# Channel mean and pointwise product of a convolution branch, from plain fp32 to rounded products of high and low parts

## The chip, the cores and the metric

One Trainium2 chip, and on it one core. The metric is the device time of one execution in microseconds (us), the median of the runs shown. A core has a matmul engine (TensorE, PE in the profile, with its weight loads as PEld), three engines for elementwise work (VectorE: DVE, ScalarE: ACT, GpSimd: POOL) and SyncE (SP), whose queue issues all transfers (DMAs) of this kernel.

## What is computed

The reference is a step of a two-layer mixer for 512 prompt tokens and 8 decoding sequences with one token each, 520 columns in all, with a model width of 1024. Each layer has a convolution branch, a pooling branch and three kinds of attention (compressed, selected, window). What matters here is the convolution branch: a depthwise convolution of width 31 over 256 channels, a layer norm over the channels, SiLU, and a pointwise product with a 256 x 256 matrix.

```python
def layernorm(x, g, b):
    mu = jnp.mean(xf, axis=-1, keepdims=True)
    xc = xf - mu
    var = jnp.mean(xc * xc, axis=-1, keepdims=True)
    return (xc * lax.rsqrt(var + EPS) * g + b)

def conv_mixer(u, buf, w_dw, b_dw, ln_g, ln_b, w_pw, b_pw):
    y = lax.conv_general_dilated(xcat, w_dw[:, None, :], ...)
    y = layernorm(y + b_dw, ln_g, ln_b)
    y = jax.nn.silu(y) @ w_pw + b_pw

def mixer_output(...):
    y = jnp.concatenate([y_a * jax.nn.silu(z_a), y_b * jax.nn.silu(z_b), o * jax.nn.silu(z_c)], axis=-1)
    return x + (y @ w_out)
```

## The kernel before

Activations lie with channels on the 128 partitions and the 520 tokens in columns, so a tile is 128 x 520, and 256 channels are two tiles. A matmul works on half of the columns, 260 (`HALF`).

The kernel has two forms of product. The large ones (`product`, lines 744 to 753; 24 per layer for the input projection, 8 for the output) are *rounded*: each operand is split into a high part, which is a copy in the rounded format fp32r, and a low part, the rest (`split`, lines 724 to 726, two operations). A burst of six matmuls then forms high x high, high weight x low activation and low weight x high activation, for both halves of the columns. The small ones, among them both products of the convolution branch, are plain fp32: one matmul per half, no split. In the trace a plain fp32 matmul stands as two records, a rounded one as one.

`conv_norm` (lines 1070 to 1101) is the branch behind the convolution. The channel mean is a product with `mean_w`, a fixed tile filled with 1/256, so that each partition gets the mean of all 256 channels; it takes one burst of two matmuls for each of the two channel tiles. The mean is subtracted, the square summed over channels by another product, the reciprocal root formed and spread by a DMA over DRAM, then come scale, tanh (for SiLU) and the pointwise product: two output tiles `m`, two channel tiles `c`, a burst of two matmuls each.

Which engine runs which elementwise operation, and in which order all of it is issued, is written out in the table `TUNE`. Wherever the program calls `ch("svg").copy(...)` and the like, the next letter of the string `engines` names the engine: `v` VectorE, `s` ScalarE, `g` GpSimd (756 letters). The program first writes down all its instructions, in bursts that stay together, and numbers the bursts as they come; the list `order` (3309 numbers) then says in which order they are issued. Each engine takes its own in that order, and a tile's place is taken from the tiles that are free at that point, so a late reader holds back a later writer. SP's transfers are in the same list.

Step names in this document are those of the program's list of steps per layer: `k`, `v` and `q` are projections to keys, values and queries, `za` and `zc` gates, `w` the output projection, `cn` is `conv_norm`. The warm-up products are in `constants` (lines 629 to 633): 12 bursts of two plain matmuls of `mean_w` with itself, whose result nobody reads. Their numbers are 3 to 14; the memset of `mean_w` is 2, the eight loads of x are 16 to 23, and 35 is the square of the first tile of x, 36 the sum of it on TensorE.

Of the kernel before, what the change touches and what calls it, by code (L numbers as in the profile page):

```python
# [9 lines left out]
F32R = mybir.dt.float32r  # L10
# [179 lines left out]
class Plan:  # L190
# [135 lines left out]
    def emit(self, tc, ctx):  # L326
# [60 lines left out]
        "vvvvgvvsssssvssgsvvggvggsvsvvssvvsgvvssvsvggsvvvgvgssgsggvvvgvsgsgsgvvggvvvsvvvvvssvsvsvsgggsvvvsvsgvgvsvgvgvssv"  # L387
        "vvsgsgsvssgvvsggsvgvsgsvsvggsvsggsvvggvggggvvssgvsssvsvsvggvvsgsgvggvvgvvgsssssggggssssvssssssvgvvggvvsvsvsgsgvv"
        "vsvvsvgsvvgvggssvvssvsvvvsvgvggggsgsvvgggggsvgvgvsssgvssvsssssvssssvsssgggvvvggsvgvvvvgvgsssssvvssvvsvvsgvvggsgg"
        "ggvggvvgvgsvvvvgsgsvvvsvgvsvsgvgsgsvsvsvsvggsvsgssggssvsvvvgvvgvgvggsvvsssvsvsssvssvgvvsssggggggvgvvvgsgsvvgssvg"  # L390
        "vsvgvsvvgsvssggvvsvgvvgvvggvsvvvvsvgvgvssvggsvvvsvssvgvsgvggvgsvggsgsgsgvgggvsggggvvvssgsvsvvsvsvsgggsgggvggvggs"
        "gsggssggssssvgsssvsvssvsgggsgvvsggvggvggvsggvssvsgvsgggssssvssvsvvvsssgvvggvggsgvvsssgggvgvgvsssssssssvsvvsvvsss"
        "sgvgvgvgvgvgvvvggvssvvvvssgvsvsvvsggvsgggvvsgsggvvsgsvgvsgggsggvsgggsgsgsvsvsvsvggvv"
    ),
    "order": (
# [146 lines left out]
def step_kernel(ctx: ExitStack, tc: tile.TileContext, i, o, tune=None):  # L542
# [82 lines left out]
    def constants():  # L625
        ve.memset(ones, 1.0)
        sc.activation(junk, ones[:, :1], AF.Exp)
        ve.memset(mean_w, 1.0 / 256.0)
        warm = plan.bank("warm", "t")
        for n in range(WARM // 2):  # L630
            with plan.burst():
# [85 lines left out]
    def layer(l):  # L717
        z_ = Layer()
# [824 lines left out]
```

## Time and profile before

| | us |
|---|---|
| median of 3 runs | 624.89 (624.7 to 625.42) |
| the profiled execution | 623.73 |
| its span, first to last instruction | 622.0 |
| TensorE busy in it | 606.4 |
| VectorE busy | 433.7 |
| ScalarE busy | 259.7 |
| GpSimd busy | 226.2 |

The profile shows one execution. An engine's busy time is that in which at least one of its instructions ran; matmuls overlap, so the time from the start of one row to the start of the next tells more than a row's own length. All rows have the line L352, the helper that issues every operation, so they are told apart by engine, names and shapes: `banks` is a result of TensorE, `t` a tile in the pools, `keep` a fixed tile, `small` a small one.

### The profile page before, as it was taken

How to read it: one execution, taken by the hardware profiler on the slowest of the kernel's cores; microseconds unless marked ns; L12 is line 12 of the kernel's file. 1: busy time of each engine (PE TensorE's matmuls, PEld its weight loads, DVE VectorE, ACT ScalarE, POOL GpSimd, SP SyncE). 2: the span in 40 equal slices, each digit the busy share in tenths (PEclk: the TensorE clock that was granted, in tenths of full speed). 3: DMA queues.
4: the chain of work that ended last, by engine and by line, in shares of the span. 5: the costliest groups of instructions: out<-in, count | busy, mean ns of one | idle time of the engine just before them, and what ended most of it. 6: DMA issues, size and time to landing. Idle time of an engine off the chain costs nothing.

```text
span 622.0 us, 15002 instructions
## 1 busy us (share of the span) xinstructions
PE 606.4 (97%) x5526; PEld 536.7 (86%) x5526; DVE 433.7 (70%) x1222; ACT 259.7 (42%) x731; POOL 226.2 (36%) x250
## 2 busy tenths in 40 slices
PE   6999999999999999999999999999999999999997
PEld 5999998898868788579999999999985968677997
DVE  6535879966778697965465498887677678688221
ACT  4102125656683395431221132237575769543100
POOL 2123225442414363341522242556443535144700
PEclk9999999999999999999999999999999999999999
DMA  8755444322652346887546234342246135788622
GB/s 267 217 166 180 152 124 146 115 76 73 136 122 65 104 125 220 268 252 228 185 143 194 85 113 160 94 124 62 77 79 155 37 95 140 185 255 252 208 77 95
DMA packets 89130, 90.98 MB, mean 146 GB/s; under 512 B 25858, under 2 KB 59746, under 8 KB 88930
## 3 DMA queue, kind: packets, MB, share of 16 engines
q1 hardware_dynamic: 89058, 90.04, 48.9%
q8 instruction: 43, 0.70, 0.5%
q14 instruction: 29, 0.24, 0.1%
HBM read 75.32 MB, written 14.67 MB: 145 GB/s over the span
## 4 chain that ended last, share of the span: by engine, by line
PE 84%; DVE 6%; SPq 5%; DMA 3%; issue 2%; ACT 1%; ACTq 0%; DVEq 0%
PE banks L352 84%; DVE t L352 4%; SPq L352 3%; DVE small L352 2%; DMA t<-in_win 2%; SPq L616 1%; ACT t L352 1%; DMA t<-in_x 1%; DMA t<-in_cmp 0%; DVE keep L352 0%; ACTq L352 0%; DVEq L352 0%
## 5 line engine op out<-in xcount | busy, mean ns | idle before, releaser
L352 PE MATMUL banks<-t,t 128*128 128x260 f32 (+5 forms) x3960 | 490.0, 302 | 1.9 <-DVE t L352 0.8
L352 PEld LDWEIGHTS banks<-t,t 128*128 128x128 f32 (+3 forms) x3960 | 434.2, 178 | 32.8 <-issue 25.1
L352 POOL TENSOR_TENSOR t<-t,t 128x512 fp32r<-128x512 f32 (+4 forms) x84 | 111.4, 1332 | 129.2 <-PE banks L352 55.7
L352 ACT ACTIVATE t<-t 128x512 fp32r<-128x512 f32 (+4 forms) x130 | 78.5, 613 | 155.1 <-DVE t L352 56.8
L352 ACT ACTIVATE t<-t,small 128x384 f32<-128x384 f32 (+4 forms) x185 | 99.2, 552 | 16.2 <-DVE small L352 15.9
L352 PE MATMUL banks<-keep,t 128*128 128x128 f32 (+7 forms) x698 | 87.2, 311 | 1.9 <-DVE t L352 1.1
L352 DVE TENSOR_TENSOR t<-t,t 128x512 fp32r<-128x512 f32 (+3 forms) x92 | 71.0, 782 | 22.0 <-PE banks L352 16.0
L352 PEld LDWEIGHTS banks<-keep,t 128*128 128x128 f32 (+2 forms) x698 | 66.5, 161 | 22.1 <-issue 12.5
L352 DVE TENSOR_TENSOR t<-banks,t 128x520 f32<-128x520 f32 (+1 forms) x54 | 37.2, 693 | 63.8 <-PE banks L352 51.2
L352 DVE CUSTOM_DVE_ANT_0 t<-banks,keep,small 128x384 f32<-128x384 f32 (+3 forms) x128 | 64.3, 528 | 16.2 <-PE banks L352 16.0
L352 POOL TENSOR_SCALAR t<-t 128x512 fp32r<-128x512 f32 (+2 forms) x49 | 34.6, 707 | 88.3 <-PE banks L352 48.5
L352 ACT ACTIVATE t<-banks 128x512 f32<-128x512 f32 (+3 forms) x72 | 36.6, 525 | 62.1 <-PE banks L352 45.7
L352 PE MATMUL banks<-t,keep 128*32 128x130 f32 (+7 forms) x688 | 41.2, 306 | 6.7 <-DVE keep L352 4.8
L352 PEld LDWEIGHTS banks<-t,keep 128*32 128x32 f32 (+3 forms) x688 | 23.2, 116 | 20.5 <-DVE keep L352 5.0
L352 POOL TENSOR_SCALAR t<-t,small 128x384 f32<-128x384 f32 (+3 forms) x50 | 32.9, 671 | 21.2 <-DVE small L352 15.4
L352 ACT ACTIVATE small<-small 128x32 f32<-128x32 f32 (+3 forms) x76 | 23.5, 310 | 27.5 <-DVE small L352 27.4
L352 DVE COPY t<-banks 128x512 f32<-128x512 f32 (+2 forms) x37 | 21.5, 589 | 11.2 <-PE banks L352 7.3
L352 DVE SCALAR_TENSOR_TENSOR t<-t,t 128x520 f32<-128x520 f32 (+2 forms) x32 | 27.8, 873 | 1.3 <-ACT t L352 1.1
L352 POOL TENSOR_TENSOR t<-t,keep 128x520 f32<-128x520 f32 (+1 forms) x11 | 14.2, 1296 | 33.5 <-DVE t L352 20.4
L352 POOL TENSOR_TENSOR t<-t 128x520 f32<-128x520 f32 (+1 forms) x12 | 12.8, 1068 | 33.2 <-DVE t L352 13.9
L352 ACT ACTIVATION_READ_ACCUMULATOR t<-t,small 128x1 f32 x132 | 24.7, 187 | 0.0
L352 DVE SCALAR_TENSOR_TENSOR small<-small 128x130 f32<-128x130 f32 (+3 forms) x80 | 23.5, 296 | 1.5
(81 smaller groups left out, 358.1 us busy)
## 6 DMA issues: line engine op xcount, KB each, us to landing
t<-in_w_in SPq DMA_DIRECT2D x96, 256.0 KB
t<-in_cmp SPq DMA_DIRECT2D x64, 128.0 KB
t<-in_slc SPq DMA_DIRECT2D x64, 128.0 KB
t<-in_w_out SPq DMA_DIRECT2D x32, 256.0 KB
t<-in_x SPq DMA_DIRECT2D x16, 260.0 KB
t<-in_win SPq DMA_DIRECT2D x16, 256.0 KB
out_win<-t SPq DMA_DIRECT2D x16, 256.0 KB
t<-glu SPq DMA_DIRECT2D x12, 264.0 KB
```

Source lines behind the costliest of these rows:

```text
L352: fn(*[real(v) for v in o.a], **{k: real(v) for k, v in o.k.items()})
L616: pages[n] = tc.nc.sync.value_load(pt.real(plan)[0:1, n:n + 1], min_val=0, max_val=n_phys - 1)
```

## The change

Both products of the branch are made rounded ones. For the mean, 1/256 is exact in the rounded format, so there is one weight tile, `mean_r` (a copy of `mean_w`), and two passes, for the high and the low part of the activations: four matmuls of 260 columns per channel tile in place of two. For the pointwise product the weights and the activations after SiLU are split, and a burst of six matmuls takes the place of two. That adds per layer five splits: the weights, two activation tiles ahead of the mean and two ahead of the pointwise product, 10 elementwise operations with a letter each. With `mean_r`, the numbers of all bursts after 2 rise by one; the warm-up bursts are now 4 to 15.

Both lists are written anew: `engines` (now 776 letters) with v 315 (before 274), s 256 (251), g 205 (231), and `order` (3330 numbers). The new order begins with the memset of `mean_w` and has eleven of the twelve warm-up bursts ahead of every other work of TensorE; the number of transfers is the same, 473.

```diff
     "order": (
-        "78 16 35 0 36 15 27 33 17 79 2 3 4 18 34 37 80 19 39 81 84 22 40 5 6 21 115 38 82 43 57 47 20 44 48 7 41 85 59 "
...
+        "2 4 5 17 6 7 16 79 36 8 81 9 34 10 116 35 82 0 11 12 13 28 18 14 118 119 38 39 19 40 20 42 43 37 48 85 24 370 21 "
...
+    mean_r = new("c", [128, 128], F32R, fixed=True)
...
         ve.memset(mean_w, 1.0 / 256.0)
+        ve.tensor_copy(mean_r, mean_w)
...
         def conv_norm():
             yv = z_.conv
+            z_.cy = []
             raw = new("wpw", [128, 2, 256])
             ld(raw, i["w_pw"][l])
+            wh, wl = (new("wpw", [128, 2, 256], F32R) for u in "hl")
+            split(raw, wh, wl, "gv")
             pm = plan.bank("pm", "mm", 2)[:, :, :T // 2]
             for c in range(2):
+                parts = [P("cy", F32R) for u in "hl"]
+                split(yv[c], *parts)
                 with plan.burst():
-                    for k, (a, b) in enumerate(HALF):
-                        te.matmul(pm[:, k], mean_w, yv[c][:, a:b], start=(c == 0), stop=(c == 1))
+                    for n, v in enumerate(parts):
+                        for k, (a, b) in enumerate(HALF):
+                            te.matmul(pm[:, k], mean_r, v[:, a:b], start=(c == n == 0), stop=(c == n == 1))
...
                 ve.scalar_tensor_tensor(yv[c], t, 1.0, yv[c], op0=OP.add, op1=OP.mult)
+                parts = [P("cy", F32R) for u in "hl"]
+                split(yv[c], *parts)
+                z_.cy.append(parts)
             for m in range(2):
                 pm = plan.bank("pm", "mm", 2)[:, :, :T // 2]
-                for c in range(2):
+                for c, (yh, yl) in enumerate(z_.cy):
                     with plan.burst():
-                        for k, (a, b) in enumerate(HALF):
-                            te.matmul(pm[:, k], raw[:, c, 128 * m:128 * m + 128], yv[c][:, a:b], start=(c == 0), stop=(c == 1))
+                        for n, (w, v) in enumerate(((wh, yh), (wh, yl), (wl, yh))):
+                            for k, (a, b) in enumerate(HALF):
+                                te.matmul(pm[:, k], w[:, c, 128 * m:128 * m + 128], v[:, a:b],
+                                          start=(c == n == 0), stop=(c == 1 and n == 2))
                 finish(m, pm, pcol(V_BPW + m), OP.add)
```

## Rows read from the trace of the kernel before

**Rows 1.** The page: busy time of each engine, and the chain that ended last.

```profile
PE 606.4 (97%) x5526; PEld 536.7 (86%) x5526; DVE 433.7 (70%) x1222; ACT 259.7 (42%) x731; POOL 226.2 (36%) x250
...
PE 84%; DVE 6%; SPq 5%; DMA 3%; issue 2%; ACT 1%; ACTq 0%; DVEq 0%
```

**Rows 2.** Busy time by stretch: stretch, its us, engines (instructions), clock, DMA share, GB/s.

```profile
8.00:11.00 3.00, 3.00 (x19) 2.15 (x19) 3.00 (x5) 1.27 (x2) 2.62 (x2) 1.00 1.02 363
...
61.00:93.00 32.00, 31.99 (x268) 31.33 (x266) 26.43 (x68) 7.13 (x17) 8.66 (x11) 1.00 0.48 145
93.00:125.00 32.00, 30.58 (x308) 27.57 (x309) 29.74 (x110) 19.07 (x56) 16.48 (x16) 1.00 0.41 127
...
340.00:430.00 90.00, 90.00 (x805) 85.69 (x804) 72.46 (x221) 28.61 (x85) 37.49 (x35) 1.00 0.36 115
```

**Rows 3.** PE's timeline at the start: start, us, shape, count, idle before and its releaser.

```profile
4.82 0.66 PE L352 MATMUL banks<-t,keep 128*32 128x130 f32 x8 [4.82 <-DVE keep L352]
...
9.02 0.66 PE L352 MATMUL banks<-t,keep 128*32 128x130 f32 x8
9.61 1.75 PE L352 MATMUL banks<-keep 128*128 128x128 f32 x8
11.28 0.65 PE L352 MATMUL banks<-t,keep 128*32 128x130 f32 x16
...
12.33 1.68 PE L352 MATMUL banks<-t,t 128*128 128x260 f32 x12
...
18.12 0.61 PE L352 MATMUL banks<-keep 128*128 128x128 f32 x4
18.48 1.68 PE L352 MATMUL banks<-t,t 128*128 128x260 f32 x12
...
31.62 0.43 PE L352 MATMUL banks<-t,keep 128*32 128x130 f32 x8 [1.03 <-POOL t L352]
32.68 10.33 PE L352 MATMUL banks<-t,t 128*128 128x160 f32 x82 [0.64 <-DMA t<-in_cmp_w]
```

**Rows 4.** DVE's timeline at the start, and SP's issues (us of issuing).

```profile
4.03 0.70 DVE L352 TENSOR_TENSOR t<-t 128x520 f32<-128x520 f32 x1 [4.03 <-DMA t<-in_x]
...
5.11 0.17 DVE L352 MEMSET keep<- 128x128 f32 x1
...
0.75 0.39 SPq L352 DMA_DIRECT2D t<-in_w_in  x1
...
33.51 7.12 SPq L352 DMA_DIRECT2D t<-in_cmp  x7
```

**Rows 5.** PE's timeline at the mean (layer one) and the pointwise product (layer two).

```profile
197.95 1.92 PE L352 MATMUL banks<-t,keep 128*128 128x260 f32 x8
199.80 0.96 PE L352 MATMUL banks<-keep,t 64*128 64x512 f32 x6
...
530.15 1.04 PE L352 MATMUL banks<-t,t 128*128 128x260 f32 x4
531.03 1.04 PE L352 MATMUL banks<-keep,t 128*128 128x128 f32 x8
```

**Rows 6.** PE's timeline: rounded products alone and in a long run.

```profile
446.85 0.96 PE L352 MATMUL banks<-t,t 128*128 128x260 f32 x6
447.65 0.60 PE L352 MATMUL banks<-keep,t 128*128 128x128 f32 x4
...
576.90 41.23 PE L352 MATMUL banks<-t,t 128*128 128x260 f32 x342
```

**Rows 7.** Groups by form, DVE and POOL: count, busy us, mean ns, idle before.

```profile
L352 DVE TENSOR_TENSOR t<-t,t 128x512 fp32r<-128x512 f32 x76 | 60.6, 804 | 21.8 <-PE banks L352 16.0 <-POOL t L352 3.1 <-issue 1.2
...
L352 DVE CAST t<-t 128x512 fp32r<-128x512 f32 x27 | 12.4, 464 | 4.0 <-DMA t<-in_w_in 3.6 <-PE banks L352 0.3
...
L352 POOL TENSOR_TENSOR t<-t,t 128x512 fp32r<-128x512 f32 x68 | 91.9, 1355 | 116.0 <-PE banks L352 55.3 <-ACT t L352 33.2 <-DVE t L352 16.5
```

**Rows 8.** The last piece of the chain: start, us, what.

```profile
618.17 0.70 DVE t L352
```

More of the change, by code (lines that the diff above doesn't have):

```diff
@@ L386 @@
     "engines": (
[L387 to L393, printed above, removed]
+        "vsssvvssgsssgssssvsgsgvvsgvgsvsssvgvvsgvvgggssvvvssvgvsvvvvvsvvvvvsvvvvvgvvsvvvvvssgggsvvvvgsggvsvssgvvsvsgsgssg"
+        "vvsgggsvssvvvsggsvsvvgsvsvsvggsgssvggvvvggsssgsvvsvsvggvgggsvsvvvvgsvsvsgvgsvggsvvgggssssssvsvvggsggvsgggggvsgsg"
+        "gvssvgvgvgsvsgvsvsvvssssssssgvgsvsvgvgvvvvvgvvvvgvssggggsgsvsgsvgvsssvssvsssssssssgsggvvvgvvvggvvvssvvsvvvgsssss"
+        "vsvsvsvsgsgggsvgvgvvgvsgsvsvvvvvsgsvvgvvsvvgvvsvvvvvsssvvgvvsvgsvvsvsgvgsgvvsggvvgssvsvvvggsvvggsssvvvggggsgvvvv"
+        "svvvsvsvvsvsgvvgvvgvvssvvvvssgvvvgvvsgvvvgvsggvsvsvvvvsggvsvssvvvsvvgvgggvsvsvsgsgggvsssvgsvssvvgvvvvvsssvvvgsgg"
+        "gsvggggvgsggvvssgvvsgsvgsvvsvsssvsvggsvvgvsggvvgvgsggsvssgssgsggssssvvssssvssvvvgggsvgvggggvgsvvvsggvgggssssvgsv"
+        "svggsvvvvsssvvsvssvvssvvvgvggvvgvggvggssvssvsgsvssvssvvsggvvgvvsvgvvvvvgsgsvsgsvsvsvgvsgggsvvgsggvgvsgsg"
     ),
     "order": (
[140 rows of a table removed]
[141 rows of a table added]
     ),
```

279 rows, old and new, of the table TUNE are left out of this document.

## The prediction

> **What bounds the kernel now.** I read the page first [rows 1]. TensorE (PE) is busy 97% of the span, VectorE (DVE) 70%, ScalarE (ACT) 42%, GpSimd (POOL) 36%, and the chain of work that ended last lies on PE for 84%. So a change pays if it shortens PE's own queue or takes away one of PE's waits; work on the other engines costs something only where PE has to wait for it. "Busy" hides two things. In a long run of rounded products 342 matmuls of 260 columns take 41.23 us, 0.12 us each, or 0.72 us for a burst of six [rows 6]; near other work the same burst takes 0.80 us (446.85 to 447.65, rows 6). And the first 12 us are slow: PE does nothing for 4.82 us, and then a burst of two warm-up products (four records) takes 0.84 us (9.61 to 11.28 is two bursts), while a later one takes 0.36 us (18.12 to 18.48) [rows 3]. [...] The end is short: the last sum on DVE starts at 618.17 and takes 0.70 us, then the output is stored [rows 8]; the change leaves it alone.
>
> **The convolution branch on PE.** Its two plain fp32 products stand in the trace as two records per matmul. The channel mean is 2 bursts of 2 matmuls per layer and takes 1.85 us (197.95 to 199.80, rows 5). It becomes 8 rounded matmuls, which stand next to each other in the new order: 0.80 us for the first six and 0.24 us for two more [rows 6], 1.04 us. That saves 0.81 us per layer, 1.6 us in both. The pointwise product is 4 bursts of 2 matmuls, 0.88 us each (530.15 to 531.03, rows 5), 3.5 us per layer. It becomes 4 bursts of six, one after the other in the second layer: 0.80 + 3 x 0.72 = 2.96 us, 0.55 us less, 1.1 us in both. Together 2.7 us. If every burst stands alone at 0.80 us, the mean costs 1.07 us and the pointwise product 3.2 us, and 2.2 us are saved.
>
> [...]
>
> **The convolution branch elsewhere.** Five splits per layer are added, each a rounded copy and a subtraction: 20 operations, and one copy of 128 columns. On DVE a copy takes 0.46 and a subtraction 0.80 us, on POOL a subtraction 1.36 us [rows 7]. The string of engines is redone for all 776 choices: DVE gets 315 of them in place of 274, ACT 256 in place of 251, POOL 205 in place of 231. With the one fixed copy that is 42 operations more on DVE, at the mean of 0.46 and 0.80 about 26 us: 434 becomes 460 us, still far under PE's span, so in sum it is hidden under PE's products. Where it lies decides. The branch itself is a chain: a split stands between the convolution and the mean, and another between the SiLU and the pointwise product. Each adds about 1.3 us (0.46 + 0.80) before PE may start a burst, at four places. PE takes its queue in order, so everything behind such a burst waits as well. Before, za products and transposes of the attention stood between; they do after too (between the multiplication by the reciprocal root and the first pointwise burst 12 bursts of PE in the first layer and 25 in the second, where it was 17 and 13). Bounds: 0 and 4 x 1.3 = 5.2 us. I take 1.0 us lost, near the lower end, because in the second layer PE goes through this very stretch without a gap [rows 5].
>
> **The start.** In the order before, DVE's first instruction is the square of the first tile of x, which waits for its DMA until 4.03 us; the memset of the weights of the warm-up products stands behind it in DVE's queue, at 5.11 us [rows 4]. So PE starts at 4.82 us, and the 12 warm-up bursts stand between real bursts. In the new order that memset is the first instruction on DVE and waits for nothing, the first square goes to ACT, and 11 of the 12 warm-up bursts stand ahead of all real work on PE; x is the first load in SP's queue. PE can then start at about 1.0 us (SP starts at 0.75 us, a memset takes 0.17, rows 4). Before, the faster pace shows first at 11.28 us (16 records of sums in 0.59 us, where 8 took that at 9.02), 6.5 us after PE's first matmul [rows 3]. The same 6.5 us from 1.0 us on hold 7.7 bursts at 0.84 us; the other 3.3 at 0.36 take 1.2, so real work starts at 8.7 us, at the faster pace. Before, PE had by 12.33 us done real work that takes 4 x 0.29 + 0.80 = 2.0 us at that pace (four sums of squares and one product, rows 3). After, that is done at 10.7 us: 1.6 us ahead. Seven warm-up bursts of before lie behind 12.33 us, at 0.36 us each [rows 3]; one is left after, 2.2 us less. Sum 3.8 us. If the pace is fast at once (11 bursts in 4.0 us) the lead is 7.5 us; if data comes too late for PE to use it, 0. What speaks for data in time: among SP's first 13 loads are the same 8 tiles of x and 3 half weights, but now of three products instead of two, so that 12 bursts can run on the first four tiles. Against it: the pages of the cache go out at 1.0 us each from SP's queue [rows 4], and the last of the first 32 stands at place 65 of that queue instead of 63; no transfer leaves earlier than before from there on.
>
> The lead has to get through the stretch of the query and key projections, 61 to 125 us, where DVE is busy 56.2 of 64 us and idle 7.8 [rows 2]. Counted by step (k, v, q, zc of the first layer) DVE has 118 operations there instead of 112: 3.8 us more, and the stretch is to be 3.8 us shorter. If DVE can use all of its idle time, that just fits; if none, the whole lead is lost. I take 1.5 us lost: 2.3 us are left.
>
> **The order elsewhere.** All of PE's 1048 bursts are redealt. I counted how often a burst of a product follows something else: 148 times before, 126 times after. A first one costs 0.80 instead of 0.72 us [rows 6]; 22 x 0.08 = 1.7 us less, with 0 as the other bound, since the transposes may cost more in turn. The number of DMAs is the same (473). The new tiles (two for the weights, eight for the activations per layer) take places that loads of weights wait for; I see no price for that in the trace and put it into the range.
>
> **Sum.** 2.7 - 1.0 + 2.3 + 1.7 = 5.7 us less. The profiled execution took 623.73 us, its span 622.0 and 1.73 around it; it would be 618.0. The median of the runs lies 1.16 us above it at 624.89, and I keep that distance: 619.2 us. The own range of this case is 616.5 to 621.7.
>
> **Rivals.** *Only the branch pays*: the lead of the start is used up behind the pages and on DVE, the runs bring nothing, and 2.7 less some 0.3 of waiting are left: 622.5 us (621.7 to 624). For it: DVE's 88% in rows 2 and the unchanged queue of pages. Against it: PE's own queue is shorter in any case. *All of it*: the lead is kept whole (3.8), no split delays PE, and the two waits of 1.0 and 0.6 us at 31.62 and 32.68 [rows 3] are filled, as more products are ready then: 2.7 + 3.8 + 1.7 + 1.7 = 9.9 us, 615.0 (612 to 616.5). *DVE takes PE's place*: the 42 operations more stand in DVE's own order ahead of what PE waits for (evacuations of products, splits of queries and weights). Place: 61 to 125 us, and the ends of both layers. It makes the kernel slower by more than 0.2% from the point at which 9.5 us of the 26 are not covered (the 8.2 us that the other terms would bring and 1.25 more), 15 operations; with half uncovered, 13.3 us, it is 630 us. Against it: outside of 61 to 125 us DVE has a fifth and more of its time free (340 to 430: 72.5 of 90 us, rows 2). *It does not do what it says*: a rounded burst in place of fp32 saves next to nothing and the new order is as good as the old one: 624.9. Against it are rows 5 and 6.
>
> **How the numbers follow.** Forecast 0.50, only the branch 0.22, all of it 0.10, DVE 0.12, nothing 0.06. A difference of 0.2% is 1.25 us, about what a measurement of this kernel can tell from none: 623.64 to 626.14 is the same. Faster: 0.50 + 0.10 + 0.18 of the 0.22 = 0.78. Same: 0.04 + 0.06 = 0.10. Slower: 0.12. The range goes from 613.5 to 625.0: the forecast, the branch alone, nothing, and most of the better case; what lies beyond 625 is left out.
>
> **What would show it.** Right: the first matmul at about 1 us and the faster pace at 7 to 8; PE in the middle of real products at 10 us; 64 records of rounded matmuls in the branch in place of 48 plain ones; DVE at about 460 us and POOL down by some 20. Wrong: gaps on PE between 61 and 125 us that end with DVE, PE waiting for a split at the mean or at the pointwise product, a first product after 10 us, or warm-up bursts at the slow pace to their end.

## The result: 617.27 us

| | before | after |
|---|---|---|
| median, 4 runs of each side by side | 624.8 (624.41 to 625.42) | 617.27 (617.18 to 618.39) |
| the profiled execution | 623.73 | 617.24 |
| its span | 622.0 | 615.5 |

The ratio is 0.9883 (95% interval 0.9866 to 0.99): 7.3 us faster, 6.2 to 8.4. The forecast was 619.2, its own range 616.5 to 621.7. In the 15 runs of the changed kernel shown here and below the mean granted clock was 0.999 to 1.00, in the 45 runs of the kernel before that stand beside the experiments 0.994 to 1.00; those at 0.997 and less are longer than the others by 0 to 1.0 us in the median, so this is not where the gain lies.

The page and the last piece of the chain of the changed kernel, as in [rows 1] and [rows 8]: PE's busy time is shorter by 4.5 us though it has 16 records more, DVE has 18 us more work, POOL 20 us less. The last piece, the sum on DVE, starts 6.5 us earlier.

```profile
PE 601.9 (98%) x5542; PEld 538.0 (87%) x5542; DVE 451.9 (73%) x1264; ACT 259.6 (42%) x736; POOL 205.8 (33%) x224
```

```profile
611.68 0.70 DVE t L352
```

Windows, as in [rows 2]: stretch, its us, busy time of PE, PEld, DVE, ACT, POOL (instructions), granted clock, DMA share, GB/s. From 93 to 125 us PE had 30.58 us of work, now it has no gap; DVE has 2.5 us more to do between 61 and 125 us and PE does not wait for it.

```profile
61.00:93.00 32.00, 32.00 (x284) 30.50 (x283) 29.99 (x73) 7.79 (x17) 9.72 (x10) 1.00 0.55 173
93.00:125.00 32.00, 32.00 (x301) 30.51 (x300) 28.68 (x110) 18.52 (x59) 18.78 (x15) 1.00 0.37 122
```

PE's timeline at the start, as in [rows 3]: start, us, shape, count, idle before and its releaser. 44 records (11 warm-up bursts) from 1.06 to 7.97, then real work at once, in records: 8 of sums, 12 of products, 8 of sums, 36 of products. One warm-up burst is left, at 17.16.

```profile
1.06 6.98 PE L352 MATMUL banks<-keep 128*128 128x128 f32 x44 [1.06 <-DVE keep L352]
7.97 0.43 PE L352 MATMUL banks<-t,keep 128*32 128x130 f32 x8
8.33 1.72 PE L352 MATMUL banks<-t,t 128*128 128x260 f32 x12
9.98 0.43 PE L352 MATMUL banks<-t,keep 128*32 128x130 f32 x8
10.34 4.59 PE L352 MATMUL banks<-t,t 128*128 128x260 f32 x36
...
17.16 0.60 PE L352 MATMUL banks<-keep 128*128 128x128 f32 x4
```

DVE and SP at the start, as in [rows 4]:

```profile
0.84 0.17 DVE L352 MEMSET keep<- 128x128 f32 x1 [0.84 <-PEq L1549]
3.84 0.49 DVE L352 TENSOR_SCALAR t<-t,keep 128x520 fp32r<-128x520 f32 x1 [2.84 <-DMA keep<-in_pv]
...
7.45 0.09 DVE L352 MEMSET keep<- 128x32 f32 x1
```

```profile
0.75 0.39 SPq L352 DMA_DIRECT2D t<-in_x  x1
```

The mean in layer one and the pointwise product in layer two, as in [rows 5]. From row to row the mean takes 1.17 us (before 1.85), the four pointwise bursts 2.97 us (533.06 to 536.03). No row has a bracket: PE waits for no split. In layer one the pointwise bursts lie inside a run of 60 products, without a gap either.

```profile
193.38 1.34 PE L352 MATMUL banks<-t,keep 128*128 128x260 f32 x8
194.55 0.60 PE L352 MATMUL banks<-keep,t 128*128 128x128 f32 x4
...
533.06 3.13 PE L352 MATMUL banks<-t,t 128*128 128x260 f32 x24
536.03 0.60 PE L352 MATMUL banks<-keep,t 128*128 128x128 f32 x4
```

Groups by form. The products are 3120 records and 406.1 us here, 3104 and 413.6 us before; DVE has 80 subtractions and 40 copies where [rows 7] have 76 and 27.

```profile
L352 PE MATMUL banks<-t,t 128*128 128x260 f32 x3120 | 406.1, 287 | 0.0
```

```profile
L352 DVE TENSOR_TENSOR t<-t,t 128x512 fp32r<-128x512 f32 x80 | 57.1, 722 | 16.8 <-POOL t L352 8.7 <-issue 3.7 <-ACT t L352 2.0
L352 DVE CAST t<-t 128x512 fp32r<-128x512 f32 x40 | 17.8, 446 | 10.1 <-DMA t<-in_w_in 6.1 <-PE banks L352 3.8
```

To see where the 6.5 us of the spans lie, PE's records were laid beside the order, and each burst was given the time from its first matmul to that of the next burst, waits included. The sums fill the span:

| us | before | after | change | forecast |
|---|---|---|---|---|
| ahead of the first matmul | 4.82 | 1.06 | -3.8 | |
| twelve warm-up bursts | 6.6 | 7.3 | +0.7 | |
| the start, both together | | | -3.1 | -2.3 |
| mean, both layers | 3.7 | 2.2 | -1.5 | -1.6 |
| pointwise product, both layers | 7.0 | 5.8 | -1.2 | -1.1 |
| all other bursts | 599.9 | 599.1 | -0.8 | -0.7 (runs -1.7, splits +1.0) |
| span | 622.0 | 615.5 | -6.5 | -5.7 |

One row needs care. In layer one of the kernel before the four plain pointwise bursts, 16 records, lie in a row of 58 with 42 records of rounded products:

```profile
226.78 8.78 PE L352 MATMUL banks<-t,t 128*128 128x260 f32 x58
235.40 0.60 PE L352 MATMUL banks<-keep,t 128*128 128x128 f32 x4
```

The row takes 8.62 us (226.78 to 235.40), the rounded records 42 x 0.12 [rows 6] = 5.0 us of it; about 3.5 us are left for the four bursts, 0.88 us each, as in layer two. From first matmul to first matmul such a burst seems to take 0.68 us, because the rounded record behind it starts 0.03 us after the burst's last record and then takes 0.31 us in place of 0.12. The table gives the burst its 0.88 us; its other figures can be off by a few tenths in the same way.

The row of all other bursts holds three things. PE's waits after the first matmul grew from 6.9 to 8.7 us (+1.8). The real bursts that PE ran at the slow pace before took 3.1 us, which would be 1.5 us at the later pace (-1.5). The remaining -1.1 us are a faster pace elsewhere. So the start is worth 4.6 us on PE's queue (3.1 and 1.5), of which later waits take some back.

### The profile page after: what moved, and what is told of

Read it like the earlier page. It is cut to its first block, busy times and chain, and to the rows that moved or that the text cites. A ratio compares the mean times of both kernels' runs of the same rounds, so it can differ in the third digit from the quotient of the medians.

```text
span 615.5 us, 15050 instructions
## 1 busy us (share of the span) xinstructions
PE 601.9 (98%) x5542; PEld 538.0 (87%) x5542; DVE 451.9 (73%) x1264; ACT 259.6 (42%) x736; POOL 205.8 (33%) x224
## 4 chain that ended last, share of the span: by engine, by line
PE 49%; DVE 2%; DMA 2%; SPq 1%; ACT 1%; issue 1%; POOL 0%; DVEq 0%; POOLq 0%
PE banks L352 49%; DVE t L352 1%; DMA t<-in_win 1%; SPq L352 1%; ACT t L352 1%; DMA t<-in_w_out 1%; DVE small L352 1%; POOL t L352 0%; ACT small L352 0%; DVEq L352 0%; POOLq L352 0%
## 5 line engine op out<-in xcount | busy, mean ns | idle before, releaser
L352 PE MATMUL banks<-t,t 128*128 128x260 f32 (+5 forms) x3976 | 483.5, 300 | 2.8 <-DVE t L352 1.8
L352 POOL TENSOR_TENSOR t<-t,t 128x512 fp32r<-128x512 f32 (+4 forms) x78 | 102.2, 1315 | 161.1 <-PE banks L352 67.8
L352 ACT ACTIVATE t<-t,small 128x384 f32<-128x384 f32 (+4 forms) x188 | 100.2, 549 | 12.5 <-DVE small L352 11.4
L352 DVE TENSOR_TENSOR t<-t,t 128x512 fp32r<-128x512 f32 (+4 forms) x108 | 75.3, 708 | 19.3 <-POOL t L352 8.7
L352 PE MATMUL banks<-keep,t 128*128 128x128 f32 (+8 forms) x698 | 86.6, 311 | 2.6 <-DVE t L352 2.3
L352 PEld LDWEIGHTS banks<-keep,t 64*128 64x128 f32 (+3 forms) x698 | 66.4, 161 | 18.3 <-issue 9.5
L352 ACT ACTIVATE small<-small 128x32 f32<-128x32 f32 (+2 forms) x75 | 23.0, 309 | 18.3 <-DVE small L352 15.6
L352 DVE CAST t<-t 128x512 fp32r<-128x512 f32 (+2 forms) x48 | 20.7, 432 | 11.0 <-DMA t<-in_w_in 6.1
L352 DVE SCALAR_TENSOR_TENSOR small<-small 128x130 f32<-128x130 f32 (+3 forms) x80 | 27.7, 347 | 1.3
L352 DVE TENSOR_TENSOR small<-small 128x130 f32<-128x130 f32 (+6 forms) x66 | 26.9, 408 | 0.9
L352 ACT ACTIVATE t<-t,keep 128x520 fp32r<-128x520 f32 (+2 forms) x17 | 14.3, 842 | 25.7 <-DVE t L352 11.0
```

The source lines that it names most:

```text
L352: fn(*[real(v) for v in o.a], **{k: real(v) for k, v in o.k.items()})
```

## The experiments

They ran in three groups, each on a chip of its own. The kernel before stood at medians of 628.55, 625.07 and 625.74 us in them, so a run is told by its ratio to the runs of the kernel before beside it, with the 95% interval.

**The changed kernel again.** It is the measure for the others.

> The changed kernel itself, unchanged, as the measure for the three others of this group and for the four runs before, all of them against the kernel before: 0.988 of the kernel before. The run with fp32 in the branch stood at 0.985 and the one with the old start at 0.991: if the branch is worth 2 to 3 us, this one stands at 0.980 to 0.982 here; if it stands at 0.985 or above, the branch brings nothing in this order.

> The changed kernel, unchanged, as the measure for the three runs beside it on the same chip: 0.984 of the kernel before, a span of 615.4.

Measured: 615.49 us, ratio 0.9841 (0.9815 to 0.9867), between the two marks, and 617.18 us, 0.9874 (0.9834 to 0.9913); the profiled spans are 615.4 and 615.2. With 0.9883 of the first measurement that is 7 to 10 us faster than before. Two runs of one kernel can differ by 0.4% in the ratio, which bounds what the following can tell.

**The branch alone, in the old order.**

```diff
 "order": (
-... 975 990 920 955 1073 1080 923 1081 974 1139 1064 1074 1076 1140 ...
+... 976 991 921 956 1145 1146 1074 1081 924 1142 1143 1082 975 1144 1065 1075 1077 1147 ...
```

The code is that of the changed kernel; 1142, 1143, 1145 and 1146 are the new splits ahead of the mean, 1144 and 1147 its two bursts, 975 the evacuation of a pooling product. The numbers of the old work are one higher.

> The branch alone: both products of the branch rounded as in the changed kernel, every other instruction in the order and on the engine of the kernel before, each split issued right behind the operation that makes its source. PE as the bound: 1.5 to 2.7 us less (2.7 of PE's queue less up to 1.2 of waiting for splits), so 622.1 to 623.3 beside 624.8. Rival, the new order alone pays: 624.8 or more, as PE waits at the mean and at the pointwise product for as long as the rounded matmuls save. Rival, no room: the new tiles take places of other work, and the run is 1 us or more slower than before.

Measured: 646.62 us, ratio 1.0274 (1.0247 to 1.03), 17 us slower than before. The third theory named the sign, not the size. PE around the mean of layer one, with DVE and POOL beside it (start, us, tile, count, idle before and its releaser):

```profile
203.28 1.85 PE L352 MATMUL banks<-t,keep 128*128 128x260 f32 x8 [3.86 <-DVE t L352]
205.07 1.65 PE L352 MATMUL banks<-keep,t 64*128 64x512 f32 x6
```

```profile
199.67 0.43 DVE L352 CAST t<-t 128x520 fp32r<-128x520 f32 x1 [2.43 <-ACT t L352]
200.13 0.70 DVE L352 TENSOR_TENSOR t<-t,t 128x520 fp32r<-128x520 f32 x1
200.75 0.22 DVE L352 TENSOR_SCALAR t<-t,keep 128x8 f32<-128x8 f32 x1
201.82 0.70 DVE L352 TENSOR_TENSOR t<-t,t 128x520 fp32r<-128x520 f32 x1 [0.85 <-POOL t L352]
202.44 0.69 DVE L352 TENSOR_TENSOR t<-banks,t 128x520 f32<-128x520 f32 x1
```

```profile
201.17 0.62 POOL L352 TENSOR_SCALAR t<-t 128x520 fp32r<-128x520 f32 x1 [5.70 <-DVE t L352]
```

PE waits 3.86 us. The first split in DVE's queue is that of the tile which ACT finishes second, at 199.63, so DVE stands still for 2.43 us; behind the split stands old work that was ready: the last piece of the other tile (200.75; before, it ran at 195.85) and, behind the second subtraction, which waits 0.85 us for POOL's copy, the evacuation of a pooling product (202.44; before, 195.98). PE's mean starts when that is done. The splits' own operations are the smaller part; the larger one is what a split that is not ready holds back in its engine's queue. What came next is in the windows of that stretch (columns as above):

```profile
198.00:202.00 4.00, 1.43 (x16) 1.01 (x12) 1.45 (x4) 2.23 (x3) 0.83 (x2) 1.00 0.00 0
202.00:206.00 4.00, 2.72 (x12) 2.41 (x14) 3.15 (x7) 0.60 (x1) 0.90 (x1) 0.69 0.00 0
206.00:210.00 4.00, 4.00 (x25) 1.93 (x21) 3.98 (x10) 1.25 (x3) 0.00 (x0) 0.88 0.22 72
...
204.00:206.00 2.00, 2.00 (x10) 1.66 (x10) 1.69 (x4) 0.47 (x1) 0.00 (x0) 0.50 0.00 0
```

PE worked 1.43 of the 4 us from 198, and then the mean granted clock is 0.69 and 0.88; the window inside, 204 to 206, reads 0.50, with PE busy throughout. In the kernel before, all three windows of 4 us read 1.00. The mean, 1.17 us in the changed kernel, takes 1.79 us here (203.28 to 205.07). The second layer repeats it (0.76 from 515 to 520 us, 0.62 from 561 to 565). The loss here is thus more than the waits themselves. The 3.86 us are only the longest of many waits: after its first matmul PE waits 22.6 us in this execution and 6.9 in that of the kernel before, 11.4 us of it from 514 to 586 us (2.0 before), and its busy time is 5.4 us longer (611.8 and 606.4) though its own work is less. The 17 us are the price of this placing as a whole; how they split over the ten splits was not tested, nor whether the old order has a better place for them.

**The branch back to plain fp32, in the new order.** The code is that of the kernel before; the order is the changed kernel's without the 21 new units.

```diff
-                for n, v in enumerate(parts):
-                    for k, (a, b) in enumerate(HALF):
-                        te.matmul(pm[:, k], mean_r, v[:, a:b], ...)
+                for k, (a, b) in enumerate(HALF):
+                    te.matmul(pm[:, k], mean_w, yv[c][:, a:b], ...)
```

> The changed kernel's order and engines, with both products of the branch in plain fp32 again and the twenty split operations and the copy left out. Branch worth what the two traces show on PE (2.0 us): 619.2 beside 617.2 for the changed kernel. If the forecast's 2.7 holds: 619.9. Rival, the branch is worth nothing by itself and the order brings all of it: 617.2. Rival, the splits held DVE back somewhere: below 617.2.

> The changed kernel's order with both products of the branch in plain fp32, once more beside the changed kernel on the same chip, since the first time the two ratios (0.9854 and 0.9841) lay within each other's intervals while the spans lay 3.1 us apart. If the branch is worth what PE's rows show (mean 1.5, pointwise 0.4): 1.9 us longer than the changed kernel. If the spans are right: 3 us longer. Rival, nothing: within 0.6 us.

Measured: 620.2 us, ratio 0.9854 (0.9831 to 0.9877), and 618.05 us, 0.9876 (0.9846 to 0.9906). Beside the changed kernel in the same group it is 0.9 us longer by the medians, 1.6 us by the spans (616.8 and 615.2); the ratios (0.9876 and 0.9874) do not tell them apart. PE's rows do: the mean takes 1.75 us per layer (501.31 to 503.06) in place of 1.05 to 1.17, the four pointwise bursts in plain fp32 3.5 us (533.71 to 537.22 in layer two) in place of 2.9 to 3.0.

```profile
501.31 1.92 PE L352 MATMUL banks<-t,keep 128*128 128x260 f32 x8
503.06 1.47 PE L352 MATMUL banks<-keep,t 128*128 128x128 f32 x12
```

The group of the products, and the page's engine line:

```profile
L352 PE MATMUL banks<-t,t 128*128 128x260 f32 x3104 | 407.0, 288 | 0.0
```

```profile
PE 605.5 (98%) x5526; PEld 539.3 (87%) x5526; DVE 446.2 (72%) x1254; ACT 258.9 (42%) x735; POOL 195.1 (32%) x214
```

So the branch gives PE 2.5 us (mean 1.3, pointwise product 1.2), and 0 to 3 us of time. Without it the new order is already 8 to 9 us faster than before: the order carries nearly all of the gain. The same 3104 products that took 413.6 us before take 407.0 here. And DVE's load is 446.2 us without any split of the branch: of the 18 us that DVE gained, 12 come from the new engines of old work.

**Only the mean rounded.** The splits of the pointwise product are left out.

```diff
-            wh, wl = (new("wpw", [128, 2, 256], F32R) for u in "hl")
-            split(raw, wh, wl, "gv")
...
-                        for n, (w, v) in enumerate(((wh, yh), (wh, yl), (wl, yh))):
-                            for k, (a, b) in enumerate(HALF):
+                        for k, (a, b) in enumerate(HALF):
```

> The changed kernel with the mean rounded but the pointwise product in plain fp32 again, its three splits per layer left out (twelve operations of DVE, ACT and POOL). By PE's rows the pointwise product alone is worth 0.4 us: 0.4 us longer than the changed kernel. By the forecast 1.1 us longer. Rival, its splits cost DVE more than PE gains: up to 2 us shorter.

Measured: 618.41 us, ratio 0.9887 (0.9858 to 0.9917), beside 0.9874 for the changed kernel. That speaks against splits that cost more than they bring; 0.4 and 1.1 us cannot be told apart by time. The 0.4 us expected from PE's rows came from the row-to-row figure of 0.68 us per burst; with 0.88 us the rows give 1.2. In the profiled execution PE waits 1.55 us for DVE just ahead of the mean and 0.66 us at it (193.14 and 194.45), and the window from 195 to 198 us reads 0.50:

```profile
195.00:198.00 3.00, 3.00 (x12) 2.38 (x14) 1.91 (x4) 1.33 (x4) 0.00 (x0) 0.50 0.28 87
```

The splits ahead of the mean are the same here as in the changed kernel, in whose three profiles PE does not wait at this place. So their place has little margin.

**The start alone, in the old order.**

```diff
 "order": (
-    "78 16 35 0 36 15 27 33 17 79 2 3 4 18 34 37 80 19 39 81 84 22 40 5 6 21 ...
+    "2 3 4 5 6 7 8 9 10 11 12 13 78 16 35 0 36 15 27 33 17 79 18 34 37 80 19 39 81 84 22 40 21 ...
```

> The start alone: the kernel before with the memset of the warm-up weights as the first instruction on DVE and 11 of the 12 warm-up bursts ahead of all real work of PE; nothing else moved. If an earlier start of PE carries to the end: first matmul at about 1 us, real work from 8 us, 2.3 to 3.8 us less, 621.0 to 622.5. Rival, the lead is lost behind loads and pages by 61 us: within 0.6 us of 624.8, and PE's idle time between 28 and 61 us grows by as much as the start gains.

Measured: 628.04 us, ratio 0.9988 (0.9966 to 1.0009): no gain that can be measured. PE's first matmul is at 1.06 us and its real work at 9.07, but then it waits, three times for DVE before 20 us, and at 31.77 for 2.23 us where [rows 3] have 1.03:

```profile
12.69 0.74 PE L352 MATMUL banks<-t,t 128*128 128x260 f32 x4 [0.31 <-DVE t L352]
...
15.20 3.13 PE L352 MATMUL banks<-t,t 128*128 128x260 f32 x24 [0.31 <-DVE t L352]
18.76 5.92 PE L352 MATMUL banks<-t,t 128*128 128x260 f32 x46 [0.43 <-DVE t L352]
...
31.77 0.43 PE L352 MATMUL banks<-t,keep 128*32 128x130 f32 x8 [2.23 <-POOL t L352]
```

The window from 12 to 16 us (columns as above):

```profile
12.00:16.00 4.00, 3.38 (x48) 2.62 (x47) 4.00 (x6) 3.89 (x7) 1.79 (x3) 1.00 0.64 218
```

DVE is busy 4.00 of the 4 us from 12 (third column of busy time). So in the old order PE's early start runs into DVE's work on x and on the first weights, and later into POOL's, neither of which starts earlier than it did.

**The old start, in the new order.**

```diff
 "order": (
-    "2 4 5 17 6 7 16 79 36 8 81 9 34 10 116 35 82 0 11 12 13 28 18 14 118 119 38 39 19 ...
+    "17 16 79 36 81 34 2 116 35 82 0 28 18 118 119 38 39 19 40 20 42 43 37 48 4 5 85 24 370 21 ...
```

> The changed kernel with the start of the kernel before: the memset behind DVE's first operation on x, ten warm-up bursts behind as many real bursts of PE as they had before and two right after them. If the start is worth the 2.3 of the forecast: 619.5. If it is worth its whole lead of 3.8 us or more: 621 to 623. Rival, its lead is lost later anyway: 617.2.

Measured: 622.6 us, ratio 0.9907 (0.9881 to 0.9932), span 620.2: 1.5 to 4 us slower than the changed kernel by the ratios, 4.7 by the spans. PE starts at 6.82 us here, the twelve bursts lie among real work until 25 us, and what is lost there is not made up later. The rows with `keep` as the only input are warm-up bursts, four records each:

```profile
6.82 0.66 PE L352 MATMUL banks<-t,keep 128*32 128x130 f32 x8 [6.82 <-DVE keep L352]
7.41 2.08 PE L352 MATMUL banks<-keep 128*128 128x128 f32 x8
9.14 2.95 PE L352 MATMUL banks<-t,t 128*128 128x260 f32 x12
...
24.62 1.05 PE L352 MATMUL banks<-keep 128*128 128x128 f32 x8
```

**No warm-up bursts at all.**

```diff
-WARM = 24
+WARM = 0
```

> The changed kernel without its twelve warm-up bursts, all else in the same order. If the warm-ups only fill the time until x is there and bring the faster pace forward: real work starts at about 4.8 us, at the slow pace until some 11 us, and is then as far as the changed kernel or up to 1.5 us behind; the time is 0 to 1.5 us longer. Rival, warm-ups are dead weight on PE and the first loads come in time: 2 to 3 us shorter. Rival, without them the pace stays slow past 11 us: 3 us or more longer.

Measured: 616.15 us, ratio 0.9863 (0.9834 to 0.9891), within the changed kernel's interval. PE's start:

```profile
7.44 0.66 PE L352 MATMUL banks<-t,keep 128*32 128x130 f32 x8 [7.44 <-DVE keep L352]
8.04 2.86 PE L352 MATMUL banks<-t,t 128*128 128x260 f32 x12
10.83 0.43 PE L352 MATMUL banks<-t,keep 128*32 128x130 f32 x8
...
17.17 16.66 PE L352 MATMUL banks<-t,t 128*128 128x260 f32 x134
```

Twelve products take 2.79 us (8.04 to 10.83) at the slow pace, 1.65 us in the changed kernel; from 10.83 on the pace is the faster one. At 17.17 PE is 0.8 us behind the changed kernel (six products), and the profiled span is nevertheless 611.8 us, as of two gaps of the changed kernel (1.77 us at 34.37, 1.08 at 60.45) the first is not there and the second is 0.37 us (58.36), with a new one of 0.38 (55.11). This execution was the fastest of its six, so its span says less than the median. The twelve bursts are thus neither what brings the gain nor what costs it: it is enough that they do not stand between real bursts.

**More of PE.** Twelve more bursts in the middle of the products.

```diff
+        dum = plan.bank("dum", "t")
+        for n in range(12):
+            with plan.burst():
+                for k in range(2):
+                    te.matmul(dum[:, :128], mean_w, mean_w, start=True, stop=True)
```

> The changed kernel with twelve more warm-up bursts on PE (results read by nobody) in one stretch at about 340 us, where PE has no gap: 12 x 0.36 = 4.3 us of PE's queue. If PE's own queue sets the end from there on: 4.3 us longer. Rival, other engines or loads set the later waits, so that PE's time is partly free: 0 to 2 us longer.

Measured: 620.91 us, ratio 0.9931 (0.9907 to 0.9955): 5.4 us above the changed kernel beside it. The bursts took 5.35 us, 339.02 to 344.37:

```profile
339.02 5.52 PE L352 MATMUL banks<-keep 128*128 128x128 f32 x48
344.37 1.86 PE L352 MATMUL banks<-t,t 128*128 128x160 f32 x14
```

A microsecond of PE's queue at that place costs a microsecond by the medians; the profiled spans, 2.3 us apart, give less, but the profiled execution was the fastest of the six here and the slowest of the five of the changed kernel. The records follow each other at 0.11 us, so a burst of four takes 0.45 us and not the 0.36 of the expectation.

**More of DVE.**

```diff
+    spare = new("c", [128, 1], fixed=True)
...
+        for n in range(57):
+            ve.tensor_reduce(spare, rope[:, 0, :512], axis=AX, op=OP.add)
```

> The changed kernel with 57 more operations on DVE (a sum over 512 columns of a fixed tile into one spare column, read by nobody), one at every 53rd place of the order from the query and key projections to the end; some 0.5 us each, 26 to 34 us of DVE, as much as the 42 operations that the change added. If DVE's load is hidden as a sum: 0 to 2 us longer. Rival, DVE takes PE's place (the forecast's case of 630): half uncovered, 13 us or more longer.

Measured: 630.99 us, ratio 1.0081 (1.0053 to 1.0109): 15.5 us above the changed kernel, slower than the kernel before. The 57 operations took 38.6 us, so each microsecond of them cost 0.4, on an engine that is busy 77%. The page's engine line, the group of the added operations, and two rows of PE's timeline:

```profile
PE 610.5 (97%) x5542; PEld 542.2 (86%) x5542; DVE 486.2 (77%) x1321; ACT 259.9 (41%) x736; POOL 207.6 (33%) x224
```

```profile
L352 DVE TENSOR_REDUCE keep<-keep 128x1 f32<-128x512 f32 x57 | 38.6, 677 | 0.0
```

```profile
112.32 3.87 PE L352 MATMUL banks<-t,t 128*128 128x260 f32 x30 [1.56 <-DVE t L352]
...
198.38 0.66 PE L352 MATMUL banks<-keep,t 128*128 128x128 f32 x4 [1.45 <-DVE small L352]
```

PE now waits for DVE at many places (1.56 us at 112.32, 1.45 at 198.38, 0.66 at the mean). Its waits after the first matmul are 15.6 us where the changed kernel beside it has 8.4; the other half of the 15.5 us is busy time (610.5 and 602.1), in which two stretches have a lower clock (0.50 from 200.3 to 203.5 and from 572.3 to 575.5). The forecast's rival, DVE in PE's place, is a real mechanism of this kernel, at 0.4 us for each microsecond added; it was priced at half. That it did not come in the changed kernel because the additional work had a place in an order made for it is likely and not shown: there the work added was also less, 18 us.

**The new order without its start and without the branch.**

```diff
 "order": (
-    "78 16 35 0 36 15 27 33 17 79 2 3 4 18 34 37 80 19 39 81 84 22 40 5 6 21 ...
+    "16 15 78 35 80 33 2 115 34 81 0 27 17 117 118 37 38 18 39 19 41 42 36 47 3 4 84 23 369 ...
```

> What is left of the change without its start and without its branch: the new order behind the start, with the start of the kernel before (as in the run that put it back) and both products in plain fp32. The forecast has 1.7 us less than the kernel before from fewer beginnings of product runs. By the runs so far (6.5 in all, some 4.7 for the start and 2 to 3 for the branch): 0 to 1.2 us longer than the kernel before. Rival, the order's worth is in the rest: 3 us or more shorter than before.

Measured: 623.04 us, ratio 0.9962 (0.9941 to 0.9982): 1.1 to 3.7 us faster than before. The forecast's 1.7 lies in it; what was drawn from the runs until then, no gain or a loss, falls. Its PE starts at 7.19 us, 2.4 us later than before, and its other bursts take 596.2 us where those of before take 599.9. Waits after the first matmul are 4.3 us in this execution, 6.9 us before, so 2.7 of these 3.7 us are waits that the new order fills; 1.0 us is pace.

## Why the prediction was right, and where it was not

Of the 1.9 us between 619.2 and 617.27, 0.8 is the sum (5.7 us less, 6.5 by the two profiled executions) and 1.1 is the distance from the profiled execution to the median: 1.16 us before, carried over to the forecast, and 0.03 after. That distance is chance; executions of one kernel lie up to 7 us apart in these groups. The steps:

*The branch on PE* was sized rightly: the mean 1.6 us forecast and 1.5 measured, the pointwise product 1.1 and 1.2, together 2.7 on both sides. By the rows a pointwise burst goes from 0.88 to 0.73 us, a sixth less.

*Splits*, 1.0 us of waiting: none is seen at any of the four places. The bounds of 0 and 5.2 us held for this order alone. The run with the branch in the old order shows 3.86 us of wait at a single place, 15.7 us more of waits in all, and a lower clock (0.50 from 204 to 206 us) behind some of them. As a bound for splits whose place in the order is not known, 4 x 1.3 us was too low by far: it counted a split's own time, not what it holds back in its queue and not the clock.

*DVE's load* rose by 18 us and not by 26: the 42 operations more came at 0.43 us each and not at the mean of a copy and a subtraction.

*The start* was forecast as a lead of 3.8 us, of which 1.5 would be lost. The lead on PE's queue is 4.6 us, and by the run with the old start 1.5 to 4.7 us are left of it. Three details failed. The loss on DVE between 61 and 125 us did not happen: PE has no gap there, where it waited 1.4 us before. The waits grew elsewhere, from 2.1 to 2.9 us ahead of 61 us and from 3.3 to 5.8 behind 125. And the reason was only half of it: the early pace of PE is not what pays. The same front in the old order brings nothing, and without the warm-up bursts the time stays. What pays is then most likely that they are out of the way of real work, in an order that has 12 products ready at 8.33 us and 36 more at 10.34. Last, the 6.5 us from the first matmul to the faster pace, taken over from before, was no constant. Record by record it is 6.0 us before, 3.8, 4.5 and 5.3 us in three executions of the changed kernel, 6.1 in the run of the start alone and 3.2 without warm-up bursts. That real work began at 7.97 us was thus partly luck; in the two other executions it began at 8.32 and 8.70, and their spans (615.4 and 615.2) are no longer for it.

*The order elsewhere*, 1.7 us less from fewer beginnings of product runs: the pace outside of the start gave 1.1 us, and 1.0 in the run that has nothing else of the change, which as a whole is 1.1 to 3.7 us faster. That it comes from the beginnings was counted and not tested. In that run most of the gain are filled waits, which the forecast had put into the better rival; in the changed kernel the waits grew by 1.8 us. How the gain of the order splits into waits and pace is not settled: it differs from run to run.

So the sum came out within 0.8 us with errors that partly cancel: the lead of the start 0.8 us more than forecast, the waits 0.7 us less than the 2.5 allowed for (1.5 and 1.0), the pace elsewhere 0.6 us less.

Of the rivals, *only the branch pays* falls most clearly, from the other side than thought: the branch alone, put into the old order right behind its sources, costs 17 us, and the order without the branch brings 8 to 9. *All of it* (615.0) lies 2.3 us off; no split delays PE, but the gap at the compression was not filled and became one of 1.77 us. *DVE takes PE's place* did not come, but had about the right price when it was brought about. *It does not do what it says* falls by the rows of the mean and of the pointwise product.

What the parts are worth does not add up: start and branch are worth 0.9 to 1.1% and 0.5% when the other is missing (0.9962 against 0.9854 to 0.9876, and against 0.9907), but 0.2 to 0.7% and about 0.1% when it is there. These numbers come from different groups and have intervals of 0.2 to 0.4%, so the overlap is likely and not shown.

A start without warm-up bursts in which the memset of `ones` (DVE, 7.45 us in the changed kernel, behind a subtraction that waits for ACT) stands first might let real work begin earlier than 7.44 us. That was not tried.

## What to carry to other kernels

An operation added to a full schedule is priced by its place: the same splits brought no wait of PE that can be seen where the order was made anew around them, and cost 17 us where they were put right behind their source. DVE's idle quarter was no slack: 38.6 us more on it, evenly laid, cost 15.5 us. Where a change comes with a new order, take the order as a change of its own and forecast it first; the arithmetic on the bottleneck engine (here 2.7 us) may be the smaller part.

## What was not expected of the hardware

A wait of PE was followed by a lower clock while PE was at work again: in the branch alone PE was idle 2.6 of the 4 us from 198, and the window from 204 to 206 us, with PE busy, reads 0.50. That trace has three more such stretches, from 32.9, 517.6 and 561.9 us on; the run with more of DVE has two (200.2 and 572.2), that with only the mean rounded one (194.9). Ahead of each stand waits that add up to between 1.3 and 3.9 us. In the changed kernel a wait of 1.77 us (34.37) was not followed by one. What decides it, no run here shows.

In the profiles of the changed kernel and of the kernel before the windows read 1.00 throughout, also at the start, where the rows show PE at the slow pace: 12 records of products in 2.79 us where PE had only 8 records of sums behind it (the run without warm-up bursts, where the windows up to 32 us read 1.00 as well), 1.65 us behind 44 records of warm-up and 8 of sums (the changed kernel). At the start this figure says nothing: the traces have no entry of the granted clock ahead of 10.87 us in the kernel before, 4.87 in the changed kernel and 10.63 without warm-up bursts, the first entry reads 1.00, and a window without an entry reads 1.00. PE's records pass from 0.21 to 0.11 us each at these very times. So the 1.00 from 8 to 11 us in [rows 2] does not tell PE's pace there, and the faster pace before came at 10.87 us, inside a row, and not at 11.28.
